# Delta rule's block inverse: all four products of a layer as 64x64 blocks with zero padding, masked copies and identity columns, issued on opposite quarters of the array in turn

## The chip, the cores and the metric

The kernel runs on one core of a Trainium2 chip. The metric is the device time of one execution in microseconds (us). Five engines take part: TensorE (PE in the views, with PEld for its weight loads), VectorE (DVE), ScalarE (ACT), GpSimd (POOL), and SyncE (SP), which issues the transfers. Each engine works through its own instructions in their written order and waits where an operand is not there yet.

## What is computed

A trunk of two layers over 512 frames of width 1024. Each layer mixes the sequence with four groups of heads (retention, an LRU, latent attention and a gated delta rule), then attends to a memory of 256 rows, then runs an MLP. The change concerns the delta rule alone. It works on 16 blocks of each half of the partitions: 8 chunks of 64 frames times 4 heads are 32 systems of 64 unknowns, and 128 partitions hold two chunks at a time.

```
lower = jnp.where(strict, jnp.einsum("bhnid,bhnjd->bhnij", kb, k) * decay, 0.0)
rhs = jnp.concatenate([vb, kb * jnp.exp(gc)[..., None]], axis=-1)
sol = lax.linalg.triangular_solve(lower + jnp.eye(c, dtype=F32), rhs,
                                  left_side=True, lower=True, unit_diagonal=True)
...
_, o = lax.scan(step, state0, (cm(u), cm(w), cm(q_dec), cm(k_dec), cm(attn), g_last.transpose(2, 0, 1)))
```

## The kernel before, in words

All float32 weight products are done as three products of split operands (`mm3_cm`, tiles `wh`, `wl`, `xh`, `xl`). `wload` loads a tile of raw weights over SP, ACT rounds it to `wh`, and DVE subtracts to get `wl`. These products write PSUM banks named `pj`, or other banks in turn, and fill most of TensorE's time. A scheduler lays all instructions out on the engines by priority. The delta rule's lane comes first in priority, latent attention second (`ch` banks), and the projections (`pj`) fill what is left. The order is fixed when the program is built.

In each layer `gdn_pre` builds the unit triangular matrix of every chunk and head (`Nm`, seen as `N3`: 128 partitions, 16 blocks, 64 columns) and inverts it:

- DVE inverts the 16x16 diagonal blocks by a loop of 15 steps (a product and a reduction each), into `Us`.
- First level, from 16 to 32: for each quarter `q` of 32 partitions DVE transposes `Us` into `U3` and `U3` into `Ta`. TensorE multiplies `N3` by `Ta` in 64 products of 16x16 blocks, ACT copies the result beside identity columns (`PI`), TensorE multiplies again (64 products with 16 rows of weights and 32 columns), and ACT and DVE copy the result into `U3`.
- Second level, from 32 to 64: DVE transposes into a second `Ta`, then 32 products of 32x32 blocks, a copy into `P1`, another 32 such products, and a copy into `U3`.

A float32 product is two instructions on TensorE, so these 192 products of a layer are 384 instructions, and 768 in two layers. Products on one quarter of the array stand together: 16 in a row on quarter `q`, then the next quarter. Afterwards `scan` walks over the 8 chunks. It multiplies `X` by `U3`, makes `vn`, updates the state `S`, and each of its steps waits for the one before.

The tiles `ca`, `th`, `Us`, `Ta`, `PI` and `P1` come from a pool `g2` of four buffers, the larger ones (`R`, `DT`, `DM`, `Nm`, `at`, `Nw`, `U`) from a pool `g4` of four.

Of the kernel before, what the change touches and what calls it, by code (L numbers as in the profile page):

```python
# [11 lines left out]
F32 = mybir.dt.float32  # L12
F32R = mybir.dt.float32r
I32 = mybir.dt.int32
AF = mybir.ActivationFunctionType
# [100 lines left out]
_c = 0  # L116
for _n, _w in [("ident", 128), ("tris", 128), ("trige", 128), ("selp", 128), ("trile", 64), ("hsel", 2),
               ("ones", 2), ("invf", 32),
               ("hf", 2), ("id16", 16), ("zeta", 4), ("rdec", 2)]:
    CST[_n] = (_c, _w)  # L120
    _c += _w
NCST = _c
# [2 lines left out]
def consts():  # L125
    f = np.float32
    t = np.arange(128)
    same = (t[:, None] // 64) == (t[None, :] // 64)
    c = np.zeros((128, NCST), f)

    def put(n, v):
        o, w = CST[n]
        c[:, o:o + w] = np.asarray(v).reshape(128, w)

    put("ident", np.eye(128))
    put("tris", same & (t[:, None] > t[None, :]))
    put("trige", same & (t[:, None] <= t[None, :]))
    put("selp", np.repeat((t[:, None] // 64) == np.arange(2)[None, :], 64, axis=1))
    put("trile", (t[:, None] % 64) <= np.arange(64)[None, :])
    put("hsel", (t[:, None] // 64) == np.arange(2)[None, :])  # L140
    put("ones", np.ones((128, 2)))
    invf = np.power(np.float64(10000.0), -np.arange(32) / 32.0).astype(f)
    put("invf", np.repeat(invf[None, :], 128, axis=0))
    half = (t % 32) // 16
    put("hf", half[:, None] == np.arange(2)[None, :])
    put("id16", (t % 32)[:, None] == np.arange(16)[None, :])
    delta = np.repeat((np.arange(16)[:, None] == np.arange(32)[None, :])[None], 128, axis=0)
    j = np.arange(128)[:, None]
    d = np.arange(128)[None, :]
    ok = (d // 64) >= (j // 64)  # L150
    ret = np.zeros((128, 6, 128))
    lg = np.log1p(-np.exp2(-5.0 - np.arange(4)))
    for h in range(4):
        ret[:, h, :] = np.where(ok, np.exp(np.abs(d - j) * lg[h]), 0.0) * 0.125
        ret[64 * (h % 2):64 * (h % 2) + 64, 4 + h // 2, :] = np.exp((d + 1) * lg[h]) * 0.125
    put("zeta", np.exp((127 - j) * lg[None, :]))
    put("rdec", np.exp(128 * lg).reshape(2, 2).T[(np.arange(128) // 64)])
    return c, ret.astype(f).reshape(128, 768), delta.astype(f).reshape(128, 512)
# [8 lines left out]
def build(tc, A, out, dbg=None):  # L167
    nc = tc.nc
    V, G, ACT, PE, SP = nc.vector, nc.gpsimd, nc.scalar, nc.tensor, nc.sync
# [8 lines left out]
    def nm(s):  # L178
        uid[0] += 1
        return f"{s}_{uid[0]}"  # L180
# [12 lines left out]
    def sct():  # L193
        return bank("gd")
# [24 lines left out]
    def tt(e, o, a, b, op):  # L219
        e.tensor_tensor(o, a, b, op=op)  # L220

    def stt(o, a, s, b, op0, op1):
        V.scalar_tensor_tensor(o, a, s, b, op0=op0, op1=op1)  # L223

    def ts(e, o, a, s1, op0, s2=None, op1=None):
        if op1 is None:
            e.tensor_scalar(o, a, s1, None, op0=op0)
        else:
            e.tensor_scalar(o, a, s1, s2, op0=op0, op1=op1)  # L229

    def act(o, i, f, **k):
        ACT.activation(o, i, f, **k)  # L232

    def mm(o, l, r, st, sp, **k):
        PE.matmul(o, lhsT=l, rhs=r, start=st, stop=sp, **k)  # L235

    MU, AD, SU, MX = ALU.mult, ALU.add, ALU.subtract, ALU.max
# [11 lines left out]
    def C(n):  # L249
        o, w = CST[n]  # L250
        return cst[:, o:o + w]
# [5 lines left out]
    ident = C("ident")  # L257
# [209 lines left out]
    def layer(l):  # L467
# [11 lines left out]
        gp = stk.enter_context(tc.tile_pool(name=f"gp{l}", bufs=1, reuse_waits="tile"))  # L479

        def g4(dt=F32):
            return gp.tile([128, 1024], dt, tag="g4", name=nm("g4"), bufs=4)

        def g2(dt=F32):
            return gp.tile([128, 512], dt, tag="g2", name=nm("g2"), bufs=4)

        def o2(tag, n):
            return op.tile([128, 512], F32, tag=tag, name=nm(tag), bufs=n)
# [44 lines left out]
        s2 = [sqk[:, i * 512:i * 512 + 512] for i in range(4)] + [s2v[:, 0:512], s2v[:, 512:1024]]  # L533
# [4 lines left out]
        for i in range(6):  # L538
            ps = pg[i] if i < 4 else proj_m("gdn", i - 4, xh, xl, new=pjt)
            with lane(*GDN):  # L540
                ca = g2()
                zq.append(evz(ps, xtmp(i)))
                conv_in(zq[i], "gcw", i * 4, ca)
                th = g2()
                act(th, ca, AF.Tanh, scale=0.5)
                stt(s2[i], th, 1.0, ca, AD, MU)
                if i < 4:
                    act(zq[i], s2[i], AF.Square)
        with lane(*GDN):
# [11 lines left out]
        def gdn_pre():  # L561
# [52 lines left out]
            for t in range(TT):  # L614
                ps = sct()
                for i in range(4):
                    tr(ps[:, i * 128:(i + 1) * 128], s2[2 + i][:, t * 128:(t + 1) * 128])
                o = gp.tile([128, 8, 64], F32, tag="kv", name=nm("kv"), bufs=4)
# [4 lines left out]
            N3 = Nm.rearrange("p (a i) -> p a i", i=64)  # L623
            at3 = at.rearrange("p (a i) -> p a i", i=64)
            for hp in range(2):
# [7 lines left out]
                for e in range(2):  # L633
                    h = 2 * hp + e
                    ps3 = pse[e].rearrange("p (t a i) -> p t a i", t=TT, a=2)
# [6 lines left out]
            Nw = g4()  # L642
# [3 lines left out]
            for q in range(4):  # L646
                b = q % 2
# [6 lines left out]
            Us3 = Us.rearrange("m (r j) -> m r j", j=32)  # L654
            SP.dma_start(out=Us, in_=A["delta"])
            for c in range(14, -1, -1):
                n = 16 - c
                pr = Nw[:, 768:768 + 16 * n].rearrange("m (r j) -> m r j", j=n)
                tt(V, pr, Us3[:, :, c:16], Nd3[:, c:c + 1, c:16].to_broadcast([128, 16, n]), MU)
                V.tensor_reduce(Us3[:, :, c], pr, axis=AX.X, op=AD)  # L660
            U = g4()
            U3 = U.rearrange("p (a i) -> p a i", i=64)
            Ta = g2()
            Ta3 = Ta.rearrange("p (a i) -> p a i", i=32)
            PI = g2()
            PI3 = PI.rearrange("p (a i) -> p a i", i=32)
            G.tensor_copy(PI3[:, :, 16:32], C("id16").unsqueeze(1).to_broadcast([128, 16, 16]))
            ps = sct()
            V.memset(ps[:, 0:256], 0.0)
            ps3 = ps[:, 0:256].rearrange("p (a i) -> p a i", i=16)  # L670
            ps2 = ps[:, 256:512].rearrange("p (a i) -> p a i", i=16)
            dg = lambda q, f=0, w=32: slice(32 * (q % 2) + 16 * f, 32 * (q % 2) + 16 * f + w)
            for q in range(4):
                rw = slice(32 * q, 32 * q + 32)
                V.transpose(U3[rw, :, dg(q)].rearrange("p t (f r) -> p r f t", f=2), Us3[rw])  # L675
                V.transpose(Ta3[rw], U3[rw, :, dg(q)])
                if q % 2:
                    G.memset(U3[rw, :, 0:32], 0.0)
                rt = slice(32 * q, 32 * q + 16)
                for a in range(16):  # L680
                    mm(ps3[rt, a, :], N3[rt, a, dg(q, 1, 16)], Ta3[rt, a, 0:16], True, True)
            act(PI3[:, :, 0:16], ps3, AF.Copy)
            for q in range(4):
                rw, rt = slice(32 * q, 32 * q + 32), slice(32 * q, 32 * q + 16)
                for a in range(16):
                    mm(ps2[rw, a, :], PI3[rt, a, :], U3[rt, a, dg(q, 1, 16)], True, True)
            Ta = g2()
            Ta3 = Ta.rearrange("p (a i) -> p a i", i=32)
            for q in range(4):
                rw = slice(32 * q, 32 * q + 32)  # L690
                if q % 2:
                    act(U3[rw, :, dg(q, 1, 16)], ps2[rw], AF.Copy)
                else:
                    V.tensor_copy(U3[rw, :, dg(q, 1, 16)], ps2[rw])
                    V.transpose(Ta3[rw], U3[rw, :, 0:32])
            ps = sct()
            ps3 = ps.rearrange("p (a i) -> p a i", i=32)
            P1 = g2()
            P13 = P1.rearrange("p (a i) -> p a i", i=32)
            for p in range(2):  # L700
                ra = slice(64 * p, 64 * p + 32)
                rb = slice(64 * p + 32, 64 * p + 64)
                for a in range(16):
                    mm(ps3[rb, a, :], N3[ra, a, 32:64], Ta3[ra, a, :], True, True)
                act(P1[rb, :], ps[rb, :], AF.Copy)
            ps = sct()
            ps3 = ps.rearrange("p (a i) -> p a i", i=32)
            for p in range(2):
                ra = slice(64 * p, 64 * p + 32)
                rb = slice(64 * p + 32, 64 * p + 64)  # L710
                for a in range(16):
                    mm(ps3[ra, a, :], P13[rb, a, :], U3[rb, a, 32:64], True, True)
                act(U3[ra, :, 32:64], ps3[ra], AF.Copy)
            kq0 = g4()
            for hp in range(2):
                ps = sct()
                for t in range(TT):
                    for e in range(2):
                        i = t * 4 + 2 * hp + e
# [23 lines left out]
        with lane(*GDN):  # L743
            egl, w16, kv, U3, at3, rr3, kq = gdn_pre()
# [758 lines left out]
```

## Time and profile before

| what | value |
|---|---|
| median of 3 runs | 1652.29 us (1651.99 to 1654.4) |
| the profiled execution's own time | 1651.16 us |
| its span, first to last instruction | 1649.4 us |
| mean granted TensorE clock | 0.984 |
| TensorE busy with products | 1612.8 us, 98% of the span |
| DVE busy | 907.8 us, 55% |
| ACT busy | 681.2 us, 41% |
| POOL busy | 107.5 us, 7% |
| chain that ended last | PE 87%, DVE 8%, DMA 2%, ACT 1% |

"Busy" is the time in which at least one instruction of the engine is under way. The granted clock is 1 where TensorE has 2.4 GHz and 0.5 where it has 1.2 GHz. The chain is followed back from the last instruction, at each step to what released it.

### The profile page before, as it was taken

To read this page: it belongs to the slowest core of one execution; us is meant where nothing else is said; L and a number is where in the kernel's file an instruction comes from. 1 tells how busy PE (TensorE), PEld (TensorE's weight loads), DVE (VectorE), ACT (ScalarE), POOL (GpSimd) and SP (SyncE) were. 2 spreads that over 40 slices of the span, in tenths; PEclk is the share of its full clock that TensorE was granted. 3 is DMA by queue.
4 is the path that set the end of the run, shared out by engine and by line. 5 is a ranking of instruction groups with operands and counts; after the bars stand their busy time and mean duration, and the time that the engine had idled before them with its cause. 6 is when DMAs were issued, how large, how long until landed. Compare 5 with 4: busy or idle time off the path is not lost.

```text
span 1649.4 us, 23179 instructions
## 1 busy us (share of the span) xinstructions
PE 1612.8 (98%) x9176; PEld 1345.8 (82%) x9176; DVE 907.8 (55%) x1949; ACT 681.2 (41%) x1169; POOL 107.5 (7%) x100
## 2 busy tenths in 40 slices
PE   6999999999999999999999999999999999999997
PEld 5868889888888888888887788998888888888886
DVE  7886588455545423443468957764573543234333
ACT  5564554344444312342335566343453442124331
POOL 2000000110010001000100000002002000100011
PEclk9997999999999999999999999999999999999998
DMA  5211134432132222333332111253312232232322
GB/s 170 85 39 34 32 102 127 140 116 89 39 102 90 102 90 91 101 97 114 115 107 67 52 40 56 84 179 115 111 43 89 90 95 97 89 102 91 101 90 77
DMA packets 47916, 150.65 MB, mean 91 GB/s; under 512 B 5696, under 2 KB 9792, under 8 KB 47808
## 3 DMA queue, kind: packets, MB, share of 16 engines
q1 hardware_dynamic: 47808, 149.17, 27.9%
q8 instruction: 72, 1.18, 0.3%
q14 instruction: 36, 0.29, 0.1%
HBM read 144.96 MB, written 4.19 MB: 90 GB/s over the span
## 4 chain that ended last, share of the span: by engine, by line
PE 87%; DVE 8%; DMA 2%; ACT 1%; issue 1%; POOL 0%; POOLq 0%; SPq 0%; ACTq 0%; DVEq 0%
PE ch L235 28%; PE pj L235 26%; PE gd L235 23%; PE lg L235 8%; DMA wr<-in_wu 2%; PE ch L403 2%; DVE wl L220 1%; ACT wh L232 1%; DVE g L649 1%; DVE xl L223 0%; DVE g L675 0%; DVE xt L220 0%; DVE rm L220 0%; DVE rw L220 0%; DVE bf L229 0%
## 5 line engine op out<-in xcount | busy, mean ns | idle before, releaser
L220 DVE TENSOR_TENSOR wl<-wr,wh 128x1024 fp32r<-128x1024 f32 (+1 forms) x256 | 310.9, 1214 | 550.3 <-PE pj L235 177.0
L232 ACT ACTIVATE wh<-wr 128x1024 fp32r<-128x1024 f32 (+1 forms) x256 | 269.7, 1054 | 635.8 <-PE pj L235 207.8
L235 PE MATMUL pj<-xh,wh 128*128 128x512 f32 x288 | 115.2, 400 | 7.2 <-ACT wh L232 7.2
L235 PE MATMUL pj<-xh,wl 128*128 128x512 f32 x288 | 115.1, 400 | 0.0
L235 PE MATMUL pj<-xl,wh 128*128 128x512 f32 x288 | 115.0, 399 | 0.0
L220 POOL TENSOR_TENSOR acc<-acc,sq 128x512 f32<-128x512 f32 x42 | 64.2, 1530 | 764.4 <-ACT sq L232 764.4
L235 PE MATMUL pj<-wl,xh 128*128 128x256 f32 (+1 forms) x352 | 107.8, 306 | 0.0
L235 PE MATMUL pj<-wh,xl 128*128 128x256 f32 (+1 forms) x352 | 107.2, 304 | 0.0
L235 PE MATMUL ch<-xh,wh 128*128 128x512 f32 x272 | 107.2, 394 | 0.0
L235 PE MATMUL ch<-xl,wh 128*128 128x512 f32 x272 | 106.7, 392 | 0.0
L235 PE MATMUL ch<-xh,wl 128*128 128x512 f32 x272 | 106.4, 391 | 0.0
L235 PE MATMUL pj<-wh,xh 128*128 128x256 f32 (+1 forms) x352 | 105.8, 301 | 0.0
L235 PE MATMUL ch<-hh,wh 128*128 128x512 f32 x192 | 75.8, 395 | 0.0
L235 PE MATMUL ch<-hl,wh 128*128 128x512 f32 x192 | 75.8, 395 | 0.0
L235 PE MATMUL ch<-hh,wl 128*128 128x512 f32 x192 | 75.8, 395 | 0.0
L235 PEld LDWEIGHTS pj<-wl,xh 128*128 128x128 f32 x352 | 69.9, 199 | 2.1 <-issue 1.1
L235 PEld LDWEIGHTS pj<-wh,xl 128*128 128x128 f32 x352 | 69.8, 198 | 1.9 <-issue 1.0
L235 PEld LDWEIGHTS pj<-wh,xh 128*128 128x128 f32 x352 | 69.9, 199 | 1.3 <-issue 0.6
L235 PEld LDWEIGHTS pj<-xh,wh 128*128 128x128 f32 x288 | 54.8, 190 | 19.2 <-ACT wh L232 7.2
L220 DVE TENSOR_TENSOR hl<-s,hh 128x512 fp32r<-128x512 f32 x64 | 44.3, 692 | 39.3 <-ACT hh L232 39.1
L235 PEld LDWEIGHTS pj<-xh,wl 128*128 128x128 f32 x288 | 54.8, 190 | 12.6 <-issue 1.0
L235 PEld LDWEIGHTS pj<-xl,wh 128*128 128x128 f32 x288 | 54.8, 190 | 12.2 <-issue 1.3
(541 smaller groups left out, 3774.0 us busy)
## 6 DMA issues: line engine op xcount, KB each, us to landing
wr<-in_wu SPq DMA_DIRECT2D x248, 512.0 KB, 3.4
x<-in_xT SPq DMA_DIRECT2D x16, 256.0 KB, 3.6
wr<-in_wu SPq DMA_DIRECT2D x8, 360.0 KB, 2.9
mem<-in_memT SPq DMA_DIRECT2D x16, 128.0 KB, 2.9
xs<-x SPq DMA_DIRECT2D x8, 256.0 KB, 2.7
x<-xs SPq DMA_DIRECT2D x8, 256.0 KB, 2.9
out<-x SPq DMA_DIRECT2D x16, 128.0 KB, 1.8
big<-in_wmla SPq DMA_DIRECT2D x2, 640.0 KB, 6.4
```

What stands on the lines that cost most here:

```text
L220: e.tensor_tensor(o, a, b, op=op)
L232: ACT.activation(o, i, f, **k)
L235: PE.matmul(o, lhsT=l, rhs=r, start=st, stop=sp, **k)
L403: PE.transpose(o, i, ident)
L649: V.transpose(Nt3[32 * q:32 * q + 32].rearrange("m j i -> m i j"), src)
```

## The change

All four products of the inverse become products of a 64x64 block (64 rows of weights, 64 columns) with 32 moving columns. One product now covers a whole chunk and head, where two or four small ones did before; the parts of the blocks that must not count are zero or are replaced by identity columns. A helper `tiles` issues 32 products for one step, and goes from the upper half of the partitions (`p` = 0) to the lower half (`p` = 1) and back after every product. A layer has four such steps, so 128 products, 256 instructions, and 512 in two layers.

To make this right, `Us` is masked into two halves by two multiplications on DVE, `U`, `Ta` and `Tb` are cleared on POOL, the identity columns of `PI` and `P1` are copied on POOL, and the first step's result is copied by a DVE multiplication with a mask `zm`. `PI` now lies in `Nw`, `Ta` and `P1` in a new single buffer `g5`. `th` is gone (the tanh is written in place) and `g2` has three buffers. The clearing of a PSUM piece and two DVE copies from PSUM are gone, and ACT copies the second step's and the fourth step's result in one instruction each.

```diff
-            return gp.tile([128, 512], dt, tag="g2", name=nm("g2"), bufs=4)
+            return gp.tile([128, 512], dt, tag="g2", name=nm("g2"), bufs=3)
...
-                th = g2()
-                act(th, ca, AF.Tanh, scale=0.5)
-                stt(s2[i], th, 1.0, ca, AD, MU)
+                act(s2[i], ca, AF.Tanh, scale=0.5)
+                stt(s2[i], s2[i], 1.0, ca, AD, MU)
...
+            g5 = lambda: gp.tile([128, 16, 64], F32, tag="g5", name=nm("g5"), bufs=1)
+            ts(V, Us3[:, :, 16:32], Us3[:, :, 0:16], C("hf")[:, 1:2], MU)
+            ts(V, Us3[:, :, 0:16], Us3[:, :, 0:16], C("hf")[:, 0:1], MU)
             U = g4()
+            G.memset(U, 0.0)
...
-            for q in range(4):
-                rw = slice(32 * q, 32 * q + 32)
-                V.transpose(U3[rw, :, dg(q)].rearrange("p t (f r) -> p r f t", f=2), Us3[rw])
-                V.transpose(Ta3[rw], U3[rw, :, dg(q)])
-                if q % 2:
-                    G.memset(U3[rw, :, 0:32], 0.0)
-                rt = slice(32 * q, 32 * q + 16)
-                for a in range(16):
-                    mm(ps3[rt, a, :], N3[rt, a, dg(q, 1, 16)], Ta3[rt, a, 0:16], True, True)
-            act(PI3[:, :, 0:16], ps3, AF.Copy)
-            for q in range(4):
-                rw, rt = slice(32 * q, 32 * q + 32), slice(32 * q, 32 * q + 16)
-                for a in range(16):
-                    mm(ps2[rw, a, :], PI3[rt, a, :], U3[rt, a, dg(q, 1, 16)], True, True)
...
+            Ta, PI = g5(), Nw.rearrange("p (a i) -> p a i", i=64)
+            G.memset(Ta, 0.0)
...
+            def tiles(o, l_, r_):
+                for a in range(16):
+                    for p in range(2):
+                        rw = slice(64 * p, 64 * p + 64)
+                        mm(o[rw, a], l_[rw, a, :], r_[rw, a], True, True)
+
+            for q in range(4):
+                rw, cb = slice(32 * q, 32 * q + 32), slice(32 * (q % 2), 32 * (q % 2) + 32)
+                V.transpose(U3[rw, :, cb].rearrange("p t (f r) -> p r f t", f=2), Us3[rw])
+                V.transpose(Ta[rw, :, cb], U3[rw, :, cb])
             ps = sct()
+            tiles(sb4(ps), N3, cut4(Ta)[:, :, :, 0, :])
+            tt(V, cut4(PI)[:, :, :, 0, :], sb4(ps),
+               C("zm").unsqueeze(1).unsqueeze(3).to_broadcast([128, 16, 2, 16]), MU)
...
+            tiles(sb4(ps), PI, cut4(U3)[:, :, :, 1, :])
+            act(cut4(U3)[:, :, :, 1, :], sb4(ps), AF.Copy)
+            Tb = g2()
+            G.memset(Tb, 0.0)
...
-                    mm(ps3[rb, a, :], N3[ra, a, 32:64], Ta3[ra, a, :], True, True)
-                act(P1[rb, :], ps[rb, :], AF.Copy)
...
+            tiles(sb3(ps), N3, Tb3)
...
+            tiles(sb3(ps), P1, U3[:, :, 32:64])
+            act(U3[:, :, 32:64], sb3(ps), AF.Copy)
```

Three places show how this moves instructions. The first is TensorE in the first layer, where the first level of the inverse begins before the change. `gd` is the bank of the delta rule, `g_152_852` is `Ta`, `g_143_753` is `Nm`, and `x16` counts 16 products in a row.

```order
L235 MATMUL pj_2049<-wh_1930,xl_132 128x256
L235 MATMUL lg_2024<-xt_2014,wlru_1856 128x512
L235 MATMUL gd_855<-g_152_852,g_143_753 16x16 x16
L235 MATMUL pj_2049<-wh_1930,xh_121 128x256
...
L235 MATMUL pj_2050<-wh_1930,xh_122 128x256
L235 MATMUL gd_855<-g_152_852,g_143_753 16x16 x16
L235 MATMUL pj_2050<-wl_1932,xh_122 128x256
```

In the changed program the same step on TensorE reads as follows (`g_146_849` is `Ta`, `g_137_747` is `Nm`).

```order
L235 MATMUL pj_1982<-wh_1863,xl_131 128x256
L235 MATMUL gd_861<-g_146_849,g_137_747 64x32
L235 MATMUL pj_1982<-wh_1863,xh_124 128x256
...
L235 MATMUL pj_1983<-wh_1863,xh_124 128x256
L235 MATMUL gd_861<-g_146_849,g_137_747 64x32 x31
L235 MATMUL pj_1983<-wl_1865,xh_124 128x256
```

Four groups of 16 small products, one for each quarter, became one lone product for the upper half and then 31 that change halves after each; 25 projection products stand between the two.

The second place is the end of the inverse on TensorE, first before the change (`g_155_996` is the second `Ta`, `g_151_851` is `U`, `g_157_1004` is `P1`).

```order
L403 MATMUL ch_1576<-cst,o_285_1556 128x128 x2
L235 MATMUL gd_1039<-g_151_851,g_157_1004 32x32 x13
L235 MATMUL gd_1003<-g_155_996,g_143_753 32x32 x16
L235 MATMUL gd_1039<-g_151_851,g_157_1004 32x32 x3
L235 MATMUL ch_1545<-o_287_1562,bf_207_1304 128x128
```

After the change the last two steps stand apart (`g_150_934` is `Tb`, `g_145_847` is `U`, `g_148_895` is `P1`).

```order
L235 MATMUL gd_938<-g_150_934,g_137_747 64x32 x31
L235 MATMUL pj_1983<-wh_1896,xh_128 128x256
L235 MATMUL pj_1983<-wl_1898,xh_128 128x256
L235 MATMUL pj_1983<-wh_1896,xl_136 128x256
L235 MATMUL ch_1559<-bf_199_1235,bf_197_1233 128x384
L235 MATMUL gd_973<-g_145_847,g_148_895 64x32
L235 MATMUL pj_2105<-wh_1986,xh_121 128x256
```

Between the third step's last product and the fourth step's first there are now four products of other work, and the copy into `P1` on ACT has to be done in their time.

The third place is DVE in the first layer, where the transposes feed the first step: before, `g_150_819` is `Us`, `g_151_851` is `U3` and `g_152_852` is `Ta`.

```order
L675 STREAM_TRANSPOSE g_151_851<-g_150_819 32x16x2x16
L223 SCALAR_TENSOR_TENSOR xt_2014<-xt_1925,par_89,xt_2014 128x511
L676 STREAM_TRANSPOSE g_152_852<-g_151_851 32x512
L223 SCALAR_TENSOR_TENSOR xt_2014<-xt_1925,par_89,xt_2014 128x510
L675 STREAM_TRANSPOSE g_151_851<-g_150_819 32x16x2x16
```

In the changed program the same transposes on DVE stand like this (`g_144_813` is `Us`, `g_145_847` is `U3`, `g_146_849` is `Ta`).

```order
L227 TENSOR_SCALAR g_144_813<-g_144_813,cst 128x16x16 x2
L223 SCALAR_TENSOR_TENSOR xt_1947<-xt_1858,par_89,xt_1947 128x511
L684 STREAM_TRANSPOSE g_145_847<-g_144_813 32x16x2x16
L223 SCALAR_TENSOR_TENSOR xt_1947<-xt_1858,par_89,xt_1947 128x510
L685 STREAM_TRANSPOSE g_146_849<-g_145_847 32x16x32
L223 SCALAR_TENSOR_TENSOR xt_1947<-xt_1858,par_89,xt_1947 128x509
L220 TENSOR_TENSOR wl_1898<-wr_1894,wh_1896 128x1024
L220 TENSOR_TENSOR xt_1924<-pj_1893,bc_370 128x512
L684 STREAM_TRANSPOSE g_145_847<-g_144_813 32x16x2x16 x2
L685 STREAM_TRANSPOSE g_146_849<-g_145_847 32x16x32
```

Before, the first small products could start after two transposes; now the first product needs four, with the two masking multiplications ahead of them, and the last row is the one that it waits for.

## Rows read from the trace of the kernel before

**Rows 1.** The page: busy us, share of the span, instructions of each engine.

```profile
PE 1612.8 (98%) x9176; PEld 1345.8 (82%) x9176; DVE 907.8 (55%) x1949; ACT 681.2 (41%) x1169; POOL 107.5 (7%) x100
```

**Rows 2.** Waits of TensorE for the inverse: us in total, times, longest.

```profile
PE gd L235 <- DVE g L676: 1.6, 2, 1.4
```

**Rows 3.** TensorE groups by form: rows*columns of weights, output, count, busy us, mean ns.

```profile
L235 PE MATMUL gd<-g,g 32*32 32x32 f32 x256 | 12.0, 215 | 0.4 <-DVE g L695 0.4
...
L235 PE MATMUL gd<-g,g 16*32 16x16 f32 x256 | 9.2, 187 | 0.0
...
L235 PE MATMUL gd<-g,g 16*16 16x16 f32 x256 | 7.8, 171 | 1.7 <-DVE g L676 1.6
```

**Rows 4.** TensorE in order of time: start, us under way, what, instructions.

```profile
124.89 0.96 PE L235 MATMUL gd<-g,g 16*16 16x16 f32 x32 [0.17 <-DVE g L676]
125.78 0.50 PE L235 MATMUL pj<-xh,wh 128*128 128x512 f32 x1
...
147.28 1.91 PE L235 MATMUL gd<-g,g 32*32 32x32 f32 x32
149.12 0.58 PE L235 MATMUL pj<-wl,xh 128*128 128x256 f32 x1
...
970.57 1.19 PE L235 MATMUL gd<-g,g 32*32 32x32 f32 x32
```

**Rows 5.** The same view, 64x64 products of the delta rule.

```profile
88.08 1.69 PE L235 MATMUL gd<-sqk 64*64 64x128 f32 x32 [0.25 <-DVE kv L220]
...
977.75 0.45 PE L235 MATMUL gd<-vn,kv 64*64 64x64 f32 x8
978.03 0.63 PE L235 MATMUL gd<-vn,g 64*64 64x64 f32 x8
978.59 0.39 PE L235 MATMUL pj<-wh,xh 128*128 128x256 f32 x1
```

**Rows 6.** TensorE by stretch: us, busy (instructions under way), granted clock, DMA share, GB/s.

```profile
85.00:95.00 10.00, 9.75 (x95) 1.00 0.00 0
...
136.50:139.90 3.40, 3.40 (x20) 0.50 0.00 0
139.90:143.30 3.40, 3.40 (x121) 1.00 0.46 154
143.30:163.80 20.50, 20.50 (x205) 0.50 0.05 15
942.03:945.45 3.42, 3.42 (x18) 0.50 0.52 153
952.27:959.10 6.83, 6.83 (x82) 0.50 0.01 2
```

**Rows 7.** TensorE in order of time: projection products at either clock.

```profile
146.51 0.41 PE L235 MATMUL pj<-wl,xh 128*128 128x256 f32 x1
146.72 0.41 PE L235 MATMUL pj<-wh,xl 128*128 128x256 f32 x1
...
976.82 0.28 PE L235 MATMUL pj<-wh,xl 128*128 128x256 f32 x1
976.94 0.28 PE L235 MATMUL pj<-wh,xh 128*128 128x256 f32 x1
```

**Rows 8.** TensorE by stretch inside a block of 16*32 products, columns as above.

```profile
950.60:950.80 0.20, 0.20 (x12) 1.00 0.29 82
951.00:951.20 0.20, 0.20 (x15) 1.00 0.00 0
```

**Rows 9.** All engines by stretch (PE, PEld, DVE, ACT, POOL, clock, DMA), and DVE's transposes.

```profile
120.00:130.00 10.00, 9.76 (x75) 6.92 (x73) 9.87 (x16) 4.80 (x9) 0.00 (x0) 1.00 0.22 62
...
125.50 1.07 DVE L675 STREAM_TRANSPOSE g<-g 32x512 f32<-32x512 f32 x1
...
129.12 0.70 DVE L676 STREAM_TRANSPOSE g<-g 32x512 f32<-32x512 f32 x1
```

**Rows 10.** POOL after its last piece of the inverse.

```profile
227.27 0.62 POOL L220 TENSOR_TENSOR xt<-xt,cst 128x256 f32<-128x256 f32 x1 [129.67 <-PE ch L403]
```

More of the change, by code (lines that the diff above doesn't have):

```diff
@@ L118 @@
                ("ones", 2), ("invf", 32),
-               ("hf", 2), ("id16", 16), ("zeta", 4), ("rdec", 2)]:
+               ("hf", 2), ("zm", 2), ("zeta", 4), ("rdec", 2)]:
     CST[_n] = (_c, _w)
@@ L145, in consts @@
     put("hf", half[:, None] == np.arange(2)[None, :])
-    put("id16", (t % 32)[:, None] == np.arange(16)[None, :])
+    put("zm", ((t % 64)[:, None] // 16) == (2 * np.arange(2) + 1)[None, :])
     delta = np.repeat((np.arange(16)[:, None] == np.arange(32)[None, :])[None], 128, axis=0)
@@ L660, in gdn_pre @@
                 V.tensor_reduce(Us3[:, :, c], pr, axis=AX.X, op=AD)
+            g5 = lambda: gp.tile([128, 16, 64], F32, tag="g5", name=nm("g5"), bufs=1)
+            ts(V, Us3[:, :, 16:32], Us3[:, :, 0:16], C("hf")[:, 1:2], MU)
+            ts(V, Us3[:, :, 0:16], Us3[:, :, 0:16], C("hf")[:, 0:1], MU)
             U = g4()
+            G.memset(U, 0.0)
             U3 = U.rearrange("p (a i) -> p a i", i=64)
-            Ta = g2()
-            Ta3 = Ta.rearrange("p (a i) -> p a i", i=32)
-            PI = g2()
@@ L666, in gdn_pre @@
-            PI3 = PI.rearrange("p (a i) -> p a i", i=32)
-            G.tensor_copy(PI3[:, :, 16:32], C("id16").unsqueeze(1).to_broadcast([128, 16, 16]))
-            ps = sct()
[L669 to L672, printed above, removed]
-            for q in range(4):
-                rw = slice(32 * q, 32 * q + 32)
-                V.transpose(U3[rw, :, dg(q)].rearrange("p t (f r) -> p r f t", f=2), Us3[rw])
-                V.transpose(Ta3[rw], U3[rw, :, dg(q)])
-                if q % 2:
-                    G.memset(U3[rw, :, 0:32], 0.0)
-                rt = slice(32 * q, 32 * q + 16)
-                for a in range(16):
-                    mm(ps3[rt, a, :], N3[rt, a, dg(q, 1, 16)], Ta3[rt, a, 0:16], True, True)
@@ L682, in gdn_pre @@
-            act(PI3[:, :, 0:16], ps3, AF.Copy)
-            for q in range(4):
-                rw, rt = slice(32 * q, 32 * q + 32), slice(32 * q, 32 * q + 16)
-                for a in range(16):
-                    mm(ps2[rw, a, :], PI3[rt, a, :], U3[rt, a, dg(q, 1, 16)], True, True)
[L687 to L695, printed above, removed]
@@ L696, in gdn_pre @@
-            ps = sct()
-            ps3 = ps.rearrange("p (a i) -> p a i", i=32)
-            P1 = g2()
-            P13 = P1.rearrange("p (a i) -> p a i", i=32)
+            Ta, PI = g5(), Nw.rearrange("p (a i) -> p a i", i=64)
+            G.memset(Ta, 0.0)
+            cut4 = lambda x: x.rearrange("p a (b f n) -> p a b f n", b=2, f=2)
+            for p in range(2):
+                rw = slice(64 * p, 64 * p + 64)
+                G.tensor_copy(cut4(PI)[rw, :, :, 1, :], ident[rw, rw].rearrange("p (b f n) -> p b f n", b=2, f=2)
+                              [:, :, 1, :].unsqueeze(1).to_broadcast([64, 16, 2, 16]))
@@ new lines, in gdn_pre @@
+            sb3 = lambda x: x.rearrange("p (a i) -> p a i", i=32)
+            sb4 = lambda x: x.rearrange("p (a b n) -> p a b n", b=2, n=16)
+            def tiles(o, l_, r_):
+                for a in range(16):
+                    for p in range(2):
+                        rw = slice(64 * p, 64 * p + 64)
+                        mm(o[rw, a], l_[rw, a, :], r_[rw, a], True, True)
[3 more added lines that the diff above has]
+                V.transpose(Ta[rw, :, cb], U3[rw, :, cb])
@@ new lines, in gdn_pre @@
+            ps = sct()
+            tiles(sb4(ps), N3, cut4(Ta)[:, :, :, 0, :])
+            tt(V, cut4(PI)[:, :, :, 0, :], sb4(ps),
+               C("zm").unsqueeze(1).unsqueeze(3).to_broadcast([128, 16, 2, 16]), MU)
+            P1 = g5()
+            for p in range(2):
+                rw = slice(64 * p, 64 * p + 64)
+                G.memset(P1[64 * p:64 * p + 32, :, 0:32], 0.0)
+                G.tensor_copy(P1[rw, :, 32:64], ident[rw, 64 * p + 32:64 * p + 64].unsqueeze(1).to_broadcast([64, 16, 32]))
@@ L700, in gdn_pre @@
+            ps = sct()
+            tiles(sb4(ps), PI, cut4(U3)[:, :, :, 1, :])
+            act(cut4(U3)[:, :, :, 1, :], sb4(ps), AF.Copy)
+            Tb = g2()
+            G.memset(Tb, 0.0)
+            Tb3 = sb3(Tb)
             for p in range(2):
                 ra = slice(64 * p, 64 * p + 32)
+                V.transpose(Tb3[ra], U3[ra, :, 0:32])
+            ps = sct()
+            tiles(sb3(ps), N3, Tb3)
+            for p in range(2):
                 rb = slice(64 * p + 32, 64 * p + 64)
-                for a in range(16):
-                    mm(ps3[rb, a, :], N3[ra, a, 32:64], Ta3[ra, a, :], True, True)
@@ L705, in gdn_pre @@
-                act(P1[rb, :], ps[rb, :], AF.Copy)
+                act(P1[rb, :, 0:32], sb3(ps)[rb], AF.Copy)
             ps = sct()
[L707 to L713, printed above, removed]
+            tiles(sb3(ps), P1, U3[:, :, 32:64])
```

## The prediction

> **What bounds the kernel now.** I read the page first: TensorE has a product under way in 98% of the span and DVE is busy for 55% [rows 1], so time goes where TensorE goes. Then the waits: for the block inverse TensorE sat idle only 1.6 us in two waits, both for a transpose on DVE [rows 2]. So the inverse costs time in three other ways: the time that its products take from the projections on the same engine, what they do to TensorE's clock, and waits that may appear. For the first I read the groups by form and the order of time; for the second the stretches with their granted clock.
>
> The reader is to see in the stretches that the clock is at 0.50 (1.2 GHz) in four of them, and that TensorE is busy all through each, 3.40 of 3.40 and 20.50 of 20.50 us [rows 6]. What it did just before: before the first, blocks of 16*16 products as the one at 124.89; before the long one, a stretch of nothing but 16*32 products, 121 under way in 3.40 us, itself still at 1.00 [rows 6]. No such stretch lies elsewhere between the start and the end of the run. The projection products show the price: one starts 0.21 us after the other at 1.2 GHz and 0.12 us at 2.4 GHz [rows 7].
>
> **The products that go.** The three groups have 768 instructions and 29.0 us of busy time [rows 3]. Busy time holds the tail of each block's last product, which runs beside the next product: the block at 124.89 is under way for 0.96 us, but the next product starts after 0.89 us [rows 4]. Counted so, from start to the start of the row behind it, the 17 blocks (from the one at 124.89 to the one at 970.57 [rows 4]) take 14.5 us in the first layer and 12.4 in the second. This removes **26.9 us**.
>
> **The products that come.** 512 instructions with 64 rows and 64 columns of weights and 32 moving columns. No row shows this form. From below: 32 instructions of 16*16 took 0.89 us, 28 ns each [rows 4], the closest spacing of small products here; it gives 14.3 us. From above, while quarters overlap: the products `vn,kv`, 64*64 with 64 moving columns and the two column halves in turn, start 8 in 0.28 us, 35 ns each [rows 5]; that gives 17.9 us. The products `sqk`, on quarters in turn, were under way for 1.69 us in a block of 32 with 128 moving columns, 53 ns [rows 5]. Without any overlap the row is `vn,g`: 8 in 0.56 us on one quarter, 70 ns [rows 5], or 35.8 us. I take 31 ns, nearest to `vn,kv` but with half its columns: **15.9 us**, so a step of 64 instructions takes 2.0 us. Net, 11.0 us go.
>
> Whether the quarters overlap is the point. The new products of both halves write one bank, on different partitions. Inside the block of 16*32 products the kernel already goes from one 32-row quarter to the next within one bank, about 32 instructions after its start at 950.16. There 15 instructions are under way in 0.2 us, and 12 in the middle of a quarter [rows 8]: starts move closer where the quarter changes. So I count on overlap.
>
> The Trainium skill speaks against this: TensorEngine Tiling (Array Packing), section Restrictions and Gotchas, says that different row tiles cannot access one PSUM bank at the same time. By that rule the new products would cost 35.8 us and the net would be 8.9 us more instead of 11.0 less. The trace disagrees as far as rows 8 go, but they show a change of quarter once in 32 instructions, not after each product, so the rule keeps a chance below.
>
> **The clock.** The four stretches at 0.50 sum to 34.1 us [rows 6]. Some 10.7 us of them are small products, already in the 26.9 (for instance the block at 147.28, 1.84 us for 32 instructions [rows 4]). The other 23.4 us would take 0.12/0.21 of that at 2.4 GHz [rows 7], 10.0 us less. Will the clock hold? For it: between 85 and 95 us TensorE runs 64*64 products on quarters in turn, the block at 88.08 among them, and the clock stays at 1.00 [rows 5, 6]. Against it: 32 moving columns are fewer than their 128, and a step stands alone for 2 us. I take **9.0 us**, which leaves one or two short stretches, and bounds of 0 and 10.0.
>
> **Waits that may come.** At 1.2 GHz the projections between two steps lasted longer and hid the hand-over to DVE or ACT. Now TensorE arrives sooner. The first product of the first step now needs four transposes instead of two, so 1.07 + 0.70 us more on DVE [rows 9], and two masking multiplications, on an engine that is busy 9.87 of 10 us there [rows 9]; the order puts the product some 5 us of projections further back in return. Queued behind it on TensorE are projections, which feed ACT and DVE. Between the third and fourth step stand four products of other work, under 1 us, for a semaphore and a copy on ACT. Bounds: 0, if all is filled, and 11 us, if each of the eight steps waits as long as the worst wait of before, 1.4 us [rows 2]. I take 0.6 us a step, **5 us**.
>
> **At nothing.** POOL clears three tiles and copies identity columns, several us a layer, but it sat idle for 129.67 us after its last piece of the inverse [rows 10], and only the clearing of `U` must come before the transposes; the copies have the first and the third step as cover. If that cover went, a copy of about 1 us would stand before a step twice a layer. ACT copies in four instructions instead of seven and DVE loses a clearing and two copies for two maskings and one larger copy: less than 1 us either way, beside TensorE's work. The missing `th` and the third `g2` buffer leave as many steps of the convolution in flight. The `delta` transfer moves ahead of three weight transfers on SP, far before its reader.
>
> **Sum.** The profiled execution's own time is 1651.2 us (its span is 1649.4, and 1.8 lie around it). 1651.2 - 26.9 + 15.9 - 9.0 + 5.0 = 1636.2. The median of the runs is 1.1 above this execution's own time, so I forecast **1637 us**.
>
> **The rivals.**
> - *The clock falls all the same.* The new steps are still small work next to a full product, and two of them within a few us may do what the 16*16 blocks did. For it: the clock has fallen in both layers, each time beside such blocks. Then the 34 us stay, half of the new steps run at 1.2 GHz (4 steps of 64 by 31 ns by 0.21/0.12 - 1, or 0.75 [rows 7]: +6 us), and waits shrink to 2: 1651.2 - 11.0 + 6 + 2, plus 1.1, is 1649. The Trainium skill, TensorE: Matmul & The Clock Gate, in the section on why this matters, ties drops of the clock to gaps in which TensorE idles; by that rule a change of block size would give nothing here. The trace disagrees: the stretch ahead of the long drop was busy 3.40 of 3.40 us [rows 6].
> - *New waits take the gain.* If DVE is later than the order assumes, TensorE stands before each step for 1 to 2 us: 14 us instead of 5 gives 1646. For it speaks DVE's 9.87 of 10 [rows 9]; against it, that waits for the inverse were 1.6 us before under the same load [rows 2].
> - *No overlap.* Both halves serialize at the shared bank: 70 ns each, 8.9 us more than before, 3.7 to 4.5 us a step, with a quarter of the array at work, so the clock falls as it does now. With 5 us of waits the time is 1651.2 + 8.9 + 5 + 1.1 = 1666. It decides from 43 ns an instruction: there, without a gain in clock, the 21.9 us left of 26.9 after waits are used up. Against it: rows 8.
> - *The change does not do what it says*, because the scheduler groups the halves again. The order shows runs of 31 and 32 products written in turn, so only a sliver is left.
>
> **Chances.** Forecast 0.60 (1630 to 1643 by its own bounds), clock falls 0.15, waits 0.12, no overlap 0.10, not in turn 0.03. The range for eight in ten goes from 1627 to 1650: down to all bounds at their best (14.3, 10.0 and no waits give 1629.7) and a little of what may go better elsewhere, up to the waits and the falling clock. Within 0.2% is about 3.3 us, what a measurement of this kernel can tell from no change. Faster: the forecast, the waits and two thirds of the falling clock, 0.82. The same: the rest of that and the last rival, 0.08. Slower: no overlap, 0.10.
>
> **What would show it.** Right: steps of 64 instructions in about 2 us, starts in pairs; a clock of 1.00 through both regions; at most a wait of about 1 us ahead of a step. Wrong in the products: spacing above 43 ns. Wrong in the clock: stretches at 0.50 right behind a step. Wrong in the waits: TensorE idle for DVE's transposes or ACT's copy into `P1` in both layers, above 10 us together.

## The result, and the profile after

The changed kernel takes 1637.95 us in the median of 5 runs (1635.19 to 1640.58), the kernel before 1651.99 us beside it: a ratio of 0.9928, 95% interval 0.9902 to 0.9954. The forecast was 1637 us. The profiled execution of the changed kernel took 1640.58 us, the longest of its five, so the sums below are made against that. Its mean granted clock is the lowest of the five too, 0.990 against 0.992 to 0.994.

The page of the changed kernel, its first row as in [rows 1]:

```profile
PE 1595.0 (97%) x8920; PEld 1330.1 (81%) x8920; DVE 905.5 (55%) x1949; ACT 679.8 (41%) x1163; POOL 116.4 (7%) x112
```

TensorE has a product under way for 17.8 us less than in [rows 1], but the span (1638.4 us) is only 11.0 shorter: the time without any product grew from 36.6 to 43.4 us. So work and clock gave more than the result shows, and waits took part of it back.

The groups of TensorE by form, where the three groups of [rows 3] have become one, and TensorE in order of time in the first layer (start, us under way, what, instructions, idle time ahead and what ended it):

```profile
L235 PE MATMUL gd<-g,g 64*64 64x32 f32 x512 | 20.4, 232 | 3.7 <-DVE g L685 2.9 <-DVE sm L893 0.7
```

```profile
135.53 0.30 PE L235 MATMUL gd<-g,g 64*64 64x32 f32 x2 [0.60 <-DVE g L685]
135.76 0.39 PE L235 MATMUL pj<-wh,xh 128*128 128x256 f32 x1
...
139.59 2.05 PE L235 MATMUL gd<-g,g 64*64 64x32 f32 x62 [0.58 <-DVE g L685]
141.57 0.39 PE L235 MATMUL pj<-wl,xh 128*128 128x256 f32 x1
...
145.50 2.06 PE L235 MATMUL gd<-g,g 64*64 64x32 f32 x64 [0.73 <-DVE sm L893]
147.48 0.44 PE L403 MATMUL ch<-cst,o 128*128 128x128 f32 x2
```

From the start of a block to the start of the row behind it, 62 instructions take 1.98 us, or 32 ns each; a lone first product takes 0.23 us. The same view in the second layer, and the stretches of it with their granted clock (us, busy, instructions, clock, DMA share, GB/s):

```profile
943.39 2.70 PE L235 MATMUL gd<-g,g 64*64 64x32 f32 x62 [1.74 <-DVE g L685]
946.02 0.58 PE L235 MATMUL pj<-wh,xh 128*128 128x256 f32 x1
...
948.45 3.63 PE L235 MATMUL gd<-g,g 64*64 64x32 f32 x64
952.00 0.58 PE L235 MATMUL pj<-wl,xh 128*128 128x256 f32 x1
```

```profile
135.00:165.00 30.00, 28.16 (x419) 1.00 0.18 55
...
941.12:944.53 3.41, 1.67 (x45) 1.00 0.46 154
944.54:947.94 3.40, 3.40 (x39) 0.50 0.00 0
947.96:951.35 3.39, 3.39 (x57) 0.50 0.31 81
951.37:954.76 3.39, 3.39 (x26) 0.50 0.01 4
954.80:965.00 10.20, 10.20 (x183) 1.00 0.25 79
```

In the first layer, where [rows 6] show 0.50 for most of the time between 136.5 and 163.8 us, the clock is at 1.00 throughout. In the second it is at 0.50 (1.2 GHz) once, for 10.2 us, and what TensorE did before was to idle for 1.74 us, for a transpose on DVE, and then begin the step at 943.39. The second step, inside that stretch, takes 3.55 us instead of 1.98.

The waits of TensorE (us in total, times, longest), beside [rows 2]:

```profile
PE gd L235 <- DVE acc L220: 6.8, 1, 6.8
PE gd L235 <- DVE g L685: 2.9, 3, 1.7
...
PE gd L235 <- DVE sm L893: 0.7, 1, 0.7
```

The last of them names a reciprocal of the attention, but the second step reads `PI`, and DVE in order of time shows the copy that writes it:

```profile
144.69 0.66 DVE L220 TENSOR_TENSOR g<-gd,cst 128x512 f32<-128x512 f32 x1
145.27 0.15 DVE L893 RECIPROCAL sm<-sm 128x1 f32<-128x1 f32 x1
```

The masked copy ends at 145.35 and the product starts at 145.50; the reciprocal merely ended in between. So three of the eight steps waited for DVE, one of them twice, 3.7 us in all. The wait for `acc` stands at 26.5 us, ahead of everything that the change touches.

### The profile page after: what moved, and what is told of

It is laid out like the page before. It is cut to its first block, busy times and chain, and to the rows that moved or that the text cites. A ratio compares the mean times of both kernels' runs of the same rounds, so it can differ in the third digit from the quotient of the medians.

```text
span 1638.4 us, 22678 instructions
## 1 busy us (share of the span) xinstructions
PE 1595.0 (97%) x8920; PEld 1330.1 (81%) x8920; DVE 905.5 (55%) x1949; ACT 679.8 (41%) x1163; POOL 116.4 (7%) x112
## 4 chain that ended last, share of the span: by engine, by line
PE 85%; DVE 8%; DMA 3%; ACT 2%; issue 1%; POOL 0%; SPq 0%; POOLq 0%; ACTq 0%; DVEq 0%
PE ch L235 28%; PE pj L235 24%; PE gd L235 23%; PE lg L235 8%; DMA wr<-in_wu 2%; DVE wl L220 1%; PE ch L403 1%; DMA mem<-in_memT 1%; ACT wh L232 1%; DVE g L648 1%; DVE g L684 0%; DVE xt L223 0%; DVE xt L220 0%; DVE bf L229 0%; DVE g L220 0%
```

## Experiments

All ran for at least 5 timed executions against the kernel before, on the same chip as that; ratios are to it.

**1. The halves apart** (the changed kernel, but 16 products of one half, then 16 of the other).

```diff
-                for a in range(16):
-                    for p in range(2):
+                for p in range(2):
+                    for a in range(16):
                         rw = slice(64 * p, 64 * p + 64)
```

> The changed kernel with the 16 products of the upper half in a row and then the 16 of the lower half, instead of in turn. Theory (products on opposite halves run beside each other, and only the turn lets them): an instruction takes about 58 ns instead of 32, a full step 3.7 us instead of 2.0, and the eight steps together cost some 13 us more; with half of the array at work for longer the clock may fall again, so 1648 to 1656 us. Rival (fewer and larger products are the gain, and the turn does nothing): steps of 2.0 us and 1635 to 1641 us.

Measured: 1669.14 us, ratio 1.0108 (1.0079 to 1.0136), profiled execution 1660.92. TensorE in order of time around a step of the first layer, and the stretches at the lower clock:

```profile
143.57 3.71 PE L235 MATMUL gd<-g,g 64*64 64x32 f32 x64
147.21 0.69 PE L403 MATMUL ch<-cst,o 128*128 128x128 f32 x2
```

```profile
147.16:150.55 3.39, 3.39 (x16) 0.50 0.21 79
154.00:171.00 17.00, 17.00 (x135) 0.50 0.05 16
959.54:969.75 10.21, 10.21 (x82) 0.50 0.09 28
980.02:983.40 3.38, 3.38 (x34) 0.50 0.00 1
```

A step of 64 takes 3.64 us, 57 ns an instruction: the same products in another order need 1.8 times as long. And the 34 us at 0.50 of [rows 6] are back, with no wait ahead of the step at 143.57 (TensorE is busy for all of the 11.0 us from 136.12 on) and the clock at 0.50 from 147.16. The theory holds in the products; in the total it was too low by some 13 us. The profiled execution is the fastest of its six, so its trace does not show what the others lost; their granted clock, 0.974 to 0.980 against its 0.983, points to more time at 1.2 GHz.

**2. The kernel before, in turn** (its own small blocks, no padding, no masks).

```diff
-                rt = slice(32 * q, 32 * q + 16)
-                for a in range(16):
+            for a in range(16):
+                for q in range(4):
+                    rt = slice(32 * q, 32 * q + 16)
                     mm(ps3[rt, a, :], N3[rt, a, dg(q, 1, 16)], Ta3[rt, a, 0:16], True, True)
...
-            for p in range(2):
-                ra = slice(64 * p, 64 * p + 32)
-                rb = slice(64 * p + 32, 64 * p + 64)
-                for a in range(16):
+            for a in range(16):
+                for p in range(2):
+                    ra = slice(64 * p, 64 * p + 32)
+                    rb = slice(64 * p + 32, 64 * p + 64)
                     mm(ps3[rb, a, :], N3[ra, a, 32:64], Ta3[ra, a, :], True, True)
```

The other two groups of products are turned in the same way.

> The kernel before with its own small blocks, but with the four quarters (first level) and the two halves (second level) in turn, after all transposes of a level. Theory (overlap is the whole of it, the size of the block does not matter): the 16*16, 16*32 and 32*32 products move from 28 to 32 ns to 8 to 16 ns an instruction, 26.9 us of small products become 8 to 14, the clock holds, and the time is 1632 to 1642 us. Rival (the clock needs more rows of the array than 16 or 32): the products shrink as well, but stretches at 0.50 of 15 us or more stay, 1641 to 1648 us. Second rival (small products are bound by their issue, 28 ns in any order): 1648 to 1655 us.

Measured: 1629.79 us (1628.76 to 1633.25), ratio 0.9880 (0.9855 to 0.9905). Groups by form, TensorE in order of time, and the two regions as stretches:

```profile
L235 PE MATMUL gd<-g,g 32*32 32x32 f32 x256 | 5.7, 192 | 0.4 <-DVE g L696 0.4
L235 PE MATMUL gd<-g,g 16*16 16x16 f32 x256 | 3.6, 176 | 2.2 <-DVE g L676 2.2
L235 PE MATMUL gd<-g,g 16*32 16x16 f32 x256 | 2.7, 180 | 1.3 <-issue 0.7 <-ACT g L232 0.6
```

```profile
134.73 1.17 PE L235 MATMUL gd<-g,g 16*16 16x16 f32 x122
135.83 0.39 PE L235 MATMUL pj<-wh,xl 128*128 128x256 f32 x1
...
145.43 1.19 PE L235 MATMUL gd<-g,g 32*32 32x32 f32 x62
146.55 0.39 PE L235 MATMUL pj<-wh,xl 128*128 128x256 f32 x1
```

```profile
120.00:165.00 45.00, 43.14 (x670) 1.00 0.18 60
915.00:960.00 45.00, 41.30 (x649) 1.00 0.18 60
```

The 768 instructions of before cost 12.0 us of busy time where [rows 3] have 29.0: 1.10 us for 122 on four quarters in turn (9 ns each), 1.12 us for 62 on two (18 ns). The clock stays at 1.00 in both regions of the profiled execution, which is the fastest of its five (granted clock 0.994, the others 0.989 to 0.993). The theory holds: the order gives the gain and needs no larger block, and this version beats both kernels; the time is even 2 us below the theory's range. Its runs and those of the changed kernel do not overlap; the two intervals of the ratios do, by 0.0003.

**3 and 4. One level alone.** First the changed kernel with the second level of before (its products, tiles and copies), then the kernel before with the second level in the new form and the buffers of run 7.

```diff
-            ps = sct()
-            tiles(sb3(ps), N3, Tb3)
+                for a in range(16):
+                    mm(ps3[rb, a, :], N3[ra, a, 32:64], Tb3[ra, a, :], True, True)
+                act(P1[rb, :], ps[rb, :], AF.Copy)
```

> The changed kernel with the second level as before (32*32 products, one half after the other). Theory: the first level holds 15.4 us of the 26.9 us of small products and costs 8.2 in the new form, and its 16-row blocks are what stands ahead of the clock's falls; so 7 us of products and most of the 9 us of the clock are gained, at about 3 us of waits: 1636 to 1643 us, at most one short stretch at 0.50. Rival (32*32 blocks pull the clock down too): stretches at 0.50 behind the second level in both layers, 1643 to 1648 us.

```diff
-                for a in range(16):
-                    mm(ps3[rb, a, :], N3[ra, a, 32:64], Ta3[ra, a, :], True, True)
-                act(P1[rb, :], ps[rb, :], AF.Copy)
+            ps = sct()
+            tiles(sb3(ps), N3, Tb3)
```

> The kernel before with the second level alone in the new form (64*64 products in turn, zeroed blocks), the first level as before; the tanh in place and three buffers as in the changed kernel. Theory: 11.5 us of small products become 8.2, a gain of 3 us, and the clock falls behind the 16-row blocks of the first level as before, 25 to 35 us at 0.50 in all: 1645 to 1651 us. Rival (the length of all small work together decides on the clock): the stretches shrink to under 15 us, 1637 to 1643 us.

Measured: 1642.55 us, ratio 0.9938 (0.9916 to 0.9960), for the first level; 1644.49 us, ratio 0.9957 (0.9940 to 0.9974), for the second. Stretches at the lower clock, of the first of the two runs and then of the second:

```profile
944.72:948.12 3.40, 3.40 (x36) 0.50 0.02 5
954.96:958.36 3.40, 3.40 (x23) 0.50 0.61 213
```

```profile
140.22:143.61 3.39, 3.39 (x27) 0.50 0.00 0
147.05:150.44 3.39, 3.39 (x17) 0.50 0.01 2
938.93:942.33 3.40, 3.40 (x35) 0.50 0.00 0
945.76:955.98 10.22, 10.22 (x116) 0.50 0.18 55
```

6.8 us stay at 0.50 with the first level new, in two stretches where at most one was expected: one behind a wait of 1.77 us and a step, the other right behind 64 of the 32x32 products at 953.01, as that run's rival had it. Six of its eleven executions took 1642.55 to 1646.40 us, with a granted clock of 0.987 or 0.988 against 0.992 in the profiled one (1638.63 us), so the clock fell for longer in them; behind which products, no trace shows. With the second level alone 20.4 us stay, between the theory's 25 to 35 and the rival's 15, and the time is 0.5 us below the theory's range. The gains, 9.6 and 7.7 us, add up to 17.3 where the whole change gave 14.0, which their spread allows.

With the second level alone new, TensorE's waits for the inverse were 0.3 us (the kernel before, with the same first level, has 2.0); with the first level new, 3.3. So the new waits belong to the first level. What part of them its masks and its four transposes have is not separated; run 2, which has no masks, waits 2.2 us for its transposes.

**5. Every step twice** (the second pass writes the same values): steps as long as in run 1, but with both halves at work.

```diff
-                for a in range(16):
+                for a in [*range(16), *range(16)]:
                     for p in range(2):
```

> The changed kernel with all 32 products of each step issued twice in a row, in turn as they are (the second pass writes the same values). Each step then lasts about 4 us, as long as in the run with the halves apart, but with both halves of the array at work. Theory (the clock falls where only a part of the array is at work for a while, not because small products last long): 512 more instructions at 29 to 32 ns add 15 to 16.5 us, and the clock behaves as in the changed kernel, at most 10 us at 0.50 in the two regions: 1650 to 1656 us. Rival (the length of a run of small products pulls the clock down): stretches at 0.50 behind several steps, as with the halves apart, 1658 to 1668 us.

Measured: 1658.79 us, ratio 1.0055 (1.0033 to 1.0076). Steps of the first layer and of the second, and the stretches:

```profile
137.83 3.92 PE L235 MATMUL gd<-g,g 64*64 64x32 f32 x126 [0.57 <-DVE g L685]
141.67 0.44 PE L403 MATMUL ch<-cst,o 128*128 128x128 f32 x2
...
947.41 6.33 PE L235 MATMUL gd<-g,g 64*64 64x32 f32 x126 [1.77 <-DVE g L685]
```

```profile
130.00:165.00 35.00, 33.80 (x652) 1.00 0.16 48
...
948.30:968.70 20.40, 20.40 (x264) 0.50 0.11 28
```

In the first layer four steps of 3.8 us, from start to start, leave the clock at 1.00, where steps of 3.6 us with the halves apart did not. The other executions agree: their granted clock is 0.984 to 0.990, and 0.974 to 0.983 with the halves apart. So the length of a step is not what brings the clock down. In the second layer it falls where it did in the changed kernel, one wait of 1.77 us and the start of a step ahead of it, and stays down for 20.4 us in place of 10.2. By starts the products take 37.9 us, 18.4 more than in the changed kernel where 15 to 16.5 were expected, since the first two steps of that layer ran mostly at 1.2 GHz. So the time is above the theory's and within the rival's range; the rival's falls behind several steps are not there.

**6. The two masks on POOL** instead of DVE.

```diff
-            ts(V, Us3[:, :, 16:32], Us3[:, :, 0:16], C("hf")[:, 1:2], MU)
-            ts(V, Us3[:, :, 0:16], Us3[:, :, 0:16], C("hf")[:, 0:1], MU)
+            ts(G, Us3[:, :, 16:32], Us3[:, :, 0:16], C("hf")[:, 1:2], MU)
+            ts(G, Us3[:, :, 0:16], Us3[:, :, 0:16], C("hf")[:, 0:1], MU)
```

> The changed kernel with the two masking multiplications of Us on POOL instead of DVE. Theory (the wait ahead of the first step, 2.9 us in three places, comes from DVE's longer chain of work, and the longest of these waits, 1.74 us, stands ahead of the clock's only fall): DVE is 1.4 us earlier in each layer, the waits fall to about 1 us, the fall of the clock in the second layer goes in most executions, 1631 to 1637 us. Rival (the scheduler's order sets the wait, and it places the products earlier too): waits and time as in the changed kernel, 1635 to 1641 us; if POOL is slow at it, up to 1643.

Measured: 1636.67 us (1635.59 to 1642.41), ratio 0.9915 (0.9883 to 0.9947), the same as the changed kernel. The groups by form show the waits:

```profile
L235 PE MATMUL gd<-g,g 64*64 64x32 f32 x512 | 18.2, 220 | 4.8 <-DVE g L685 3.9 <-DVE sm L893 0.9
```

The theory falls: the waits did not shrink, they grew from 3.7 to 4.8 us. In the first layer the lone product starts at 135.15 us and the 62 at 139.21, 0.4 us earlier than in the changed kernel, and each still waits 0.6 us for its transpose. POOL and DVE in order of time show why so little came of it:

```profile
126.65 0.92 POOL L227 TENSOR_SCALAR g<-g,cst 128x256 f32<-128x256 f32 x1
127.60 1.09 DVE L684 STREAM_TRANSPOSE g<-g 32x512 f32<-32x512 f32 x1 [1.40 <-POOL g L227]
```

In the changed kernel the two masks take 1.45 us on DVE. On POOL they take from 124.98 to 127.57, with a copy of identity columns between them, and DVE stands idle for 1.40 us until the second is done (1.83 us in the second layer). So the masks still stand ahead of the transposes, and the run does not tell what the waits would be without them. Nor did TensorE's order move much in the first layer: by the trace 600 instructions start ahead of the lone product, 601 in the changed kernel. In this execution the clock did not fall in the second layer, after waits of 1.38 and 1.35 us.

**7. The buffers alone** (the kernel before with the tanh in place and three `g2` buffers).

```diff
-                th = g2()
-                act(th, ca, AF.Tanh, scale=0.5)
-                stt(s2[i], th, 1.0, ca, AD, MU)
+                act(s2[i], ca, AF.Tanh, scale=0.5)
+                stt(s2[i], s2[i], 1.0, ca, AD, MU)
```

> The kernel before with only the in-place tanh and three g2 buffers instead of four, the inverse untouched. Theory (this part costs and gives nothing): 1650 to 1654 us. Rival (fewer buffers hold up the convolution or the inverse, or the freed order helps): outside 1648 to 1656 us.

Measured: 1650.36 us, ratio 0.9993 (0.9970 to 1.0016). This part is worth nothing that the runs can tell, as costed.

**8. The small blocks in turn, two quarters at a time** on the first level.

```diff
-            for a in range(16):
-                for q in range(4):
+            for qa, a in [(qa, a) for qa in (0, 2) for a in range(16)]:
+                for q in (qa, qa + 1):
```

> The small blocks of before in turn, but on the first level two quarters at a time (the first two, then the last two) instead of all four; the second level on two halves in turn as in the run with everything in turn. Theory (the spacing of instructions is that of one quarter, 28 to 36 ns, divided by the number of quarters in turn): a 16*16 or 16*32 instruction takes 14 to 18 ns instead of 9, the first level costs 2.5 to 4 us more, the clock holds, 1631 to 1636 us. Rival (starting the first products after half of the transposes fills the waits on DVE and gives the difference back): 1627 to 1631 us.

Measured: 1635.70 us (1634.81 to 1636.52), ratio 0.9908 (0.9880 to 0.9936). TensorE in order of time and the stretches:

```profile
134.42 0.96 PE L235 MATMUL gd<-g,g 16*16 16x16 f32 x62
135.31 0.39 PE L235 MATMUL pj<-wh,xh 128*128 128x256 f32 x1
```

```profile
120.00:136.70 16.70, 15.83 (x238) 1.00 0.19 65
136.78:143.58 6.80, 6.78 (x108) 0.50 0.01 2
938.91:945.70 6.79, 6.79 (x67) 0.50 0.02 5
```

62 instructions take 0.89 us, 14 ns each, half of the 28 on one quarter [rows 4] and more than the 9 on four. For two quarters that is the time of one divided by the number in turn; for four the division would give 7. The time is in the theory's range, but the clock did not hold: it fell beside the small blocks in both layers, 13.6 us in all, though TensorE was busy for all of the 8.9 us ahead of the second fall.

## Why the prediction was right

**The products that go.** Low by one block. By the same count, from start to start, TensorE has 18 such blocks and not 17; the 17 hold only 736 of the 768 instructions. The one left out is the first of the second layer, ahead of the wait at 938.84:

```profile
933.98 0.96 PE L235 MATMUL gd<-g,g 16*16 16x16 f32 x32
934.87 0.50 PE L235 MATMUL pj<-xh,wh 128*128 128x512 f32 x1
```

With it the second layer takes 13.3 us where 12.4 were counted, and 27.8 us go in place of 26.9. The expectations of runs 2 and 3 hold the same slip: the first level had 16.3 us, not 15.4.

**The products that come.** Right in kind, a little low. 62 instructions in 1.98 us are 32 ns, against 31 chosen. The lone first product of a step costs 0.23 us, which was not counted, and one step and a part of another ran at 1.2 GHz. By starts the 14 new blocks (the first at 135.53, the last at 961.33) take 8.6 us in the first layer and 10.8 in the second, 19.4 where 15.9 were forecast. The rival of no overlap is settled by run 1: with the halves apart an instruction takes 57 ns, in turn 32. That the kernel then takes 1669 us, near that rival's 1666, is in part chance, for 70 ns were priced. The rule of the Trainium skill that was weighed there (TensorEngine Tiling (Array Packing), Restrictions and Gotchas: different row tiles cannot access one PSUM bank at the same time) would make both orders equally long; 32 ns in turn and 57 ns apart, in the same bank, disagree.

**The clock.** Right. Of the 10.2 us at 0.50 that remain, some 5.0 lie inside the two steps, so 5.2 us of other work ran at the lower clock where 23.4 did before. By the 0.12/0.21 of [rows 7] that gives 7.8 us back; 9.0 were forecast. That the new order holds the clock rests on runs 1 and 5, which differ in what part of the array is at work while a step lasts, and so in how many products start in a microsecond; no run separates the two. The clock is the larger part of the gain: in the two executions of each kernel on record at a granted clock of 0.992, the kernel before (beside runs 5 to 7) took 1641.57 and 1643.20 us and the changed kernel 1637.95 and 1639.97. At an equal clock that leaves some 3 of the 14 us, an estimate from four executions, for products and waits together.

**The waits.** The size was near, the place was wrong. TensorE without a product grew by 6.8 us, forecast 5.0. But the prediction spread 0.6 us over each of eight steps; only three waited, all on the first level, and for the inverse the wait grew from 2.0 us [rows 2, 3] to 3.7. Another 1.5 us is the earlier wait for `acc` (5.3 us in the profile of before), and the remaining 3.6 us are many small waits on other lanes, for which no run here gives a cause. The feared copy into `P1` never showed.

**The sum.** 1651.2 - 27.8 + 19.4 - 7.8 + 6.8 = 1641.8, against the 1640.6 of the profiled execution; 1.2 us are not accounted for. The median lies 2.6 us below that execution. So the exact hit of 1637 has luck in it: the new products and the waits cost 5.3 us more than forecast and the clock gave 1.2 less, and this was met by the block left out, by the rest, and by the profiled execution being the slowest of its five where the forecast had added 1.1 us for the median. Neither the prediction nor this sum counts a stretch at 0.50 near the start, beside the wait for `acc`: 6.8 us in the kernel before (23.85 to 30.68) and 10.2 in the changed one.

**What stays open.** Why the clock falls after a wait of 1.74 us (1.77 in runs 3 and 5) and a step, and not after the waits of 0.57 to 1.38 us of the other steps, nor in run 2 after 1.49 us: the wait itself was not set by any run. TensorE: Matmul & The Clock Gate in the Trainium skill, section on why this matters, ties drops to idle gaps. The fall during the wait of 6.8 us for `acc` fits it (0.50 from 22.95 us on), the fall after 1.74 us stands behind a gap shorter than the section speaks of, and those of run 1 at 147.16 and of [rows 6] at 136.5 and 143.3 have no gap of 0.2 us or more in the 10 us ahead of them.

## What to carry to other kernels

Products that use only a part of TensorE's array should go to different row or column parts in turn, one after the other, before anybody makes them larger: the order alone was worth 22 us here, and the padded 64x64 products in turn 14. Read the price of such products by start-to-start times and by the clock behind them, because the projections that follow pay as well; and when blocks are added up, add up their instructions too. Moving a link of a chain to another engine does not shorten the chain when the engine behind it stands and waits for that link, as DVE did for POOL in run 6.

## What the hardware showed that was not expected

- Overlap needs no large block: 16*16 products on four quarters in turn start every 9 ns on average, on two every 14, on one every 28. The Trainium skill says in TensorE: Matmul & The Clock Gate, section on why this matters, that products sliced to different row groups run concurrently; the trace agrees, even within one PSUM bank.
- The granted clock fell with TensorE's products under way all through (11.0 us ahead of the first fall of run 1, 8.9 us ahead of the second of run 8), behind work on a half of the array (run 1) or on two quarters (run 8), and it did not fall for as long a step with both halves at work (run 5, first layer, 3.8 us against 3.6).
